# Layer 2's input projection taken of x times the scale, the norm's factor and the shift's product applied at its result

## The chip, the cores and the metric

The kernel runs on one core of a Trainium2 chip. The metric is device time in microseconds (us), of one launch. Engines are named as in the profile: PE (matrix multiply), PEld (PE's weight loads), DVE (vector), ACT (scalar with table functions), POOL (GpSimd), SP (the queue that issues most transfers).

## The reference

Two layers (`DEPTH` 2) over 1024 latent tokens and 256 context tokens, 1024 channels. What matters here is how a layer begins and what reads it:

```python
for l in range(DEPTH):
    sh1, sc1, g1, sh2, sc2, g2 = jnp.split(mod_l, 6, axis=-1)       # csh1, csc1, ... for the context
    hl = modulate(rms_norm(x, norm1[l]), sh1, sc1)
    hc = modulate(rms_norm(h_ctx, norm1[l]), csh1, csc1)
    y_l, y_c = token_mixers(hl, hc, ...)      # starts with hl @ w_in[l], hc @ w_in[l]
    x = x + g1 * y_l
    x = x + g2 * swiglu(modulate(rms_norm(x, norm2[l]), sh2, sc2), w_ffn_in[l], w_ffn_out[l])
    # the same for h_ctx, unless this is the last layer

qa, kva, kr, xr, gr, su, sv = split(h @ w_in)  # in token_mixers
```

`modulate(n, sh, sc)` is n (1 + sc) + sh, and `rms_norm` divides a token by the root of its mean square and multiplies by a gain. So the projection's operand is x · am · r + sh: `am`, the gain times (1 + sc), is one number per channel, `r` one per token, `sh` one per channel. From `qa` and `kva` (each normed again) come queries, keys and values of 10 heads; `xr` goes through a convolution, gates and a two-way recurrence; `gr` multiplies its result after a gelu; `su` and `sv` make a gated unit along the tokens.

## The kernel before

All arrays are fp32, and each is split into a high and a low part, so that a product is three matmuls: weights' high part (`wh`) with the operand's high and low part, and weights' low part (`wl`) with the high part. Channels lie on the 128 partitions, so x is 8 tiles (k or m) of tokens. A projection `prj` of 384 tokens is 24 matmuls of 384 columns (8 k by 3), one of 256 tokens 24 of 256.

The 1280 tokens are two chunks: chunk c=0 has tokens 0 to 640, c=1 the latent tokens 640 to 1024 (384 of them) and the 256 of the context; `SUBS` names the pieces, 384 and 256.

One program is written out by hand for all engines, with one queue per engine, in order. `pace(main)` runs a main generator, and each of its steps lets *lanes* (side generators, `Lane(gen, priority)`) go on; a model of engine clocks (`_Line`) decides how far. The order is fixed when the program is made. `ensure(condition)` runs lanes until a condition holds.

The end of layer 1 and the beginning of layer 2 (in the trace at 1646 to 1748 us):

- `ffn_rest(1, ...)`, the first pass: for each m, PE makes the last part of the feed-forward's result (`fr`, 512 latent columns and 256 of the context), DVE adds it to x (`x<-fr,g2h,x`), and `Running.add` has ACT square x (`sq`) and POOL add the squares over m; the last adds are on DVE. `ffn_rest(0, ...)`, the second pass, does the same for latent tokens 0 to 512.
- `rms_rinv`: three matmuls with ones (`ms`), then ACT (logarithm, exponential, square) and DVE (`v`, `v`, `r`) make `r`.
- `modulated`, in lanes: per k, DVE `ht` = x · am · r, ACT `h` high = `ht` + shift, DVE `h` low. There are 32 `ht` in this layer.
- `project`: PE's `prj` in the order `xr` (two output tiles of chunk 1, then two of chunk 0), `su`, `sv`, `kv`, `qa`, `gg` (the reference's gr). `sv` is made with h as the weights, so tokens lie on the partitions. ACT copies each result from PE's memory (`evac_copy`).

Behind `xr`, the recurrence (ACT gates, DVE scans) runs beside `su` and `sv`. Its last step, a DVE split of the next weights (`wl`) behind it and the first `kv` projection behind that, are at 1818.4. The low-rank norms of `kv` and `qa` (`acc`, `ms`, `v`, `r`, `kvf`, `qaf`, `qal`) lie among the `qa` and `gg` projections; then come k, v and q of the first pair of heads, and the first head's score maxima (`mx`) at 1902.5.

## Time and profile before

| | us |
|---|---|
| median of three runs | 3025.57 (3017.51 to 3028.01) |
| the profiled execution | 3020.45 |
| its span in the trace | 3018.7 |
| busy in it: PE, DVE, ACT, POOL | 2831.0, 2188.0, 1537.5, 927.5 |

The span is cut into stages by what PE does. A stage's own busy times, and what PE waits for in it, tell more than the shares of the whole span, since PE is busy almost all the time outside of a few stages.

### The profile page before, as it was taken

The numbers are of one execution on the slowest core, as the hardware profiler recorded it, in microseconds if no ns is written. First come the engines' busy times: TensorE is split into PE (matmuls) and PEld (weight loads), VectorE is DVE, ScalarE is ACT, GpSimd is POOL, SyncE is SP. The second block draws the span as 40 slices with busy tenths as digits, with TensorE's granted clock in tenths as the row PEclk, the third lists the DMA queues.
The fourth block names the chain that finished last, engine by engine and source line by source line (L and its number), as shares of the span: only waits on it lengthen the run. The fifth ranks groups of instructions, "written<-read, shape, count | busy, mean of one in ns | idle before, by whom it ended". The sixth has DMA issues, their size and how long they took to land.

```text
span 3018.7 us, 38935 instructions
## 1 busy us (share of the span) xinstructions
PE 2831.0 (94%) x13824; PEld 2316.2 (77%) x13824; DVE 2188.0 (72%) x3350; ACT 1537.5 (51%) x2846; POOL 927.5 (31%) x784
## 2 busy tenths in 40 slices
PE   6999999998899999999999799899999899999997
PEld 4788677777678788888888588577767688887886
DVE  5685777656688987776666767666756887777887
ACT  5665787874443333342112486578765544443223
POOL 0001366721223333332222200267712122222332
PEclk9999999999999999999999899999999899999999
DMA  7312000024144555558644211000024254446861
GB/s 279 127 32 78 25 18 1 1 98 156 41 149 160 187 178 199 178 186 305 258 155 152 87 47 50 25 8 8 1 96 156 67 174 150 150 150 246 326 248 66
DMA packets 150483, 378.65 MB, mean 125 GB/s; under 512 B 16016, under 2 KB 30352, under 8 KB 150288
## 3 DMA queue, kind: packets, MB, share of 16 engines
q1 hardware_dynamic: 147664, 367.24, 34.6%
q0 software_dynamic: 2624, 8.91, 0.8%
q8 instruction: 109, 1.79, 0.2%
q14 instruction: 86, 0.70, 0.1%
HBM read 270.19 MB, written 105.91 MB: 125 GB/s over the span
## 4 chain that ended last, share of the span: by engine, by line
PE 62%; DVE 14%; ACT 5%; DMA 3%; issue 2%; POOL 1%; DVEq 0%; POOLq 0%; ACTq 0%; SPq 0%
PE ffA L117 14%; PE foA L117 7%; PE ffC L117 6%; PE pv L117 5%; PE s L117 5%; PE ffB L117 3%; PE op L117 3%; PE foC L117 3%; PE prj L117 3%; DVE wl L117 2%; PE ffCU L117 2%; DVE x L117 2%; PE foX L117 2%; PE foB L117 2%; PE ffCG L117 2%
## 5 line engine op out<-in xcount | busy, mean ns | idle before, releaser
L117 DVE TENSOR_TENSOR wl<-wr,wh 128x512 fp32r<-128x512 f32 (+2 forms) x433 | 360.8, 835 | 152.6 <-ACT wh L117 150.1
L117 ACT CAST wh<-wr 128x512 fp32r<-128x512 f32 (+2 forms) x433 | 274.7, 651 | 381.4 <-PE foX L117 199.8
L117 PE MATMUL ffA<-T,wh 128*128 128x512 f32 x1056 | 334.7, 397 | 17.4 <-DVE e L117 9.1
L117 POOL TENSOR_TENSOR pl<-pf,ph 128x512 fp32r<-128x512 f32 (+1 forms) x231 | 308.7, 1346 | 137.7 <-ACT ph L117 110.5
L117 PE MATMUL prj<-h,wh 128*128 128x384 f32 (+1 forms) x1056 | 260.0, 334 | 18.5 <-ACT h L117 8.3
L117 ACT ACTIVATE pf<-s 128x512 f32<-128x512 f32 (+1 forms) x336 | 195.6, 588 | 114.6 <-PE s L117 109.8
L117 PEld LDWEIGHTS ffA<-T,wh 128*128 128x128 f32 x1056 | 199.3, 191 | 64.0 <-DVE T L117 12.3
L117 POOL TENSOR_TENSOR s<-wr 128x512 f32<-128x512 f32 (+1 forms) x84 | 93.7, 1116 | 415.2 <-DMA wr<-in_wfu_dram 191.2
L117 PEld LDWEIGHTS prj<-h,wh 128*128 128x128 f32 x1056 | 189.6, 199 | 40.6 <-DVE h L117 14.3
L117 DVE TENSOR_REDUCE mx<-mx 128x1 f32<-128x512 f32 (+1 forms) x328 | 202.9, 680 | 19.7 <-PE mx L117 19.1
L117 PE MATMUL ffA<-T,wl 128*128 128x512 f32 x528 | 208.1, 394 | 0.0
L117 ACT ACTIVATE th<-e 128x512 f32<-128x512 f32 x88 | 55.6, 632 | 272.6 <-DVE e L117 241.1
L117 PE MATMUL op<-y,wh 128*128 128x512 f32 (+1 forms) x576 | 182.6, 389 | 4.3 <-ACT y L117 2.0
L117 PE MATMUL prj<-h,wl 128*128 128x384 f32 (+1 forms) x528 | 170.9, 324 | 8.9 <-DVE wl L117 8.9
L117 DVE TENSOR_TENSOR wl<-s,wh 128x512 fp32r<-128x512 f32 (+1 forms) x168 | 158.4, 946 | 15.6 <-ACT wh L117 15.4
L117 POOL TENSOR_TENSOR sq<-sq,sq 128x512 f32<-128x512 f32 (+1 forms) x66 | 73.6, 1119 | 309.3 <-ACT sq L117 307.8
L117 POOL DMA_DIRECT2D ys<-y x20 | 11.1, 554 | 499.4 <-DVE y L117 498.6
L117 DVE SCALAR_TENSOR_TENSOR x<-foA,g2h,x 128x512 f32<-128x512 f32 x160 | 120.0, 750 | 60.4 <-PE foA L117 58.7
L117 PE MATMUL s<-qh,kh 97*128 97x512 f32 (+3 forms) x336 | 153.1, 456 | 4.0 <-ACT qh L117 1.8
L117 PE MATMUL foA<-T,wh 128*128 128x512 f32 x480 | 149.0, 392 | 6.4 <-DVE x L117 5.6
L117 ACT ACTIVATE ph<-s 128x512 fp32r<-128x512 f32 x242 | 141.6, 585 | 1.2 <-POOL qf L117 1.0
L117 PEld LDWEIGHTS op<-y,wh 128*128 128x128 f32 x576 | 109.3, 191 | 30.0 <-ACT wh L117 3.0
(348 smaller groups left out, 7889.3 us busy)
## 6 DMA issues: line engine op xcount, KB each, us to landing
wr<-in_wada_dram SPq DMA_DIRECT2D x80, 512.0 KB, 4.3
pair<-oh SPq DMA_DIRECT2D x140, 256.0 KB, 2.6
pair<-ol SPq DMA_DIRECT2D x140, 256.0 KB, 2.1
T<-pair SPq DMA_DIRECT2D x60, 512.0 KB, 9.3
wr<-in_wfg_dram SPq DMA_DIRECT2D x44, 512.0 KB, 4.1
wr<-in_wfu_dram SPq DMA_DIRECT2D x44, 512.0 KB, 5.2
wr<-in_wfo_dram SPq DMA_DIRECT2D x80, 256.0 KB, 5.0
B<-pair SPq DMA_DIRECT2D x40, 512.0 KB, 8.0
```

The lines of the kernel that those rows point to most:

```text
L117: return f(*args, **kw)
```

## The change

The high and low parts `h` of layer 2 are now made of x · am alone, by `Scaled`, inside the two passes of `ffn_rest`: one ACT operation (from x) and one DVE operation (x · am − high, with x and the high part as tensors), a step behind x. `ht` is gone. The token's factor `r` is kept in one tile `rn`. It is applied where a projection is read: DVE multiplies the result by `rn` (`pt`), and ACT adds the shift's product as a bias instead of copying. That product comes from two more columns of `h` (the shift of latent and context tokens) in the first piece of chunk 1, which is 386 columns wide; ACT copies it to `shifts`. For `sv` the factor has to lie on the partitions: ten small matmuls (`rt`) and two more `sv` tiles (`rows`, the shift's product spread over the partitions) are made, and DVE reads each tile with `stt` in place of ACT's copy. In the second pass the squares are added by DVE (`tt`), in the first still by POOL. `maxima` gives `mx` and `mr` three buffers of their own, and `next_pairs` waits for the values of the pair before.

```diff
     class Running:
         def add(self, k):
             sq = temp(name="sq")[:, : self.n]
             act(sq, x_at(k, self.g, self.n), AF.Square)
             self.flush()
...
-        def flush(self, add=gp.tensor_tensor):
+        def flush(self, add=None):
             if self.late is not None:
-                add(self.acc, self.acc, self.late, op=OP.add)
+                (add or self.how)(self.acc, self.acc, self.late, op=OP.add)
...
+    class Scaled:
+        def put(self, hs, k, pieces):
+            if len(hs) <= k:
+                hs.append(full((P, 2, CH + 2), R32, "h"))
+                if hs.second:
+                    h, b = hs[k][:, :, SHIFTS : SHIFTS + 2], self.mod[:, self.sh + k, 0:2]
+                    sc.copy(h[:, 0, :], b)
+                    self.late.append((tt, (h[:, 1, :], b, h[:, 0, :]), dict(op=OP.subtract)))
+            for at, n, g, w in pieces:
+                u = at_column(hs, at)
+                h, x, a = hs[k][:, :, u : u + n], x_at(k, g, n), self.am[:, k, w : w + 1]
+                act(h[:, 0, :], x, AF.Identity, scale=a)
+                self.late.append((stt, (h[:, 1, :], x, a, h[:, 0, :]), dict(op0=OP.mult, op1=OP.subtract)))
...
+            def late(ps, g, n):
+                if g == CH:
+                    sc.copy(shifts[:, of : of + 2], ps[:, n : n + 2])
+                t, v = temp(name="pt"), 0
+                while v < n:
+                    r, m = factor(g + v, n - v)
+                    tt(t[:, v : v + m], ps[:, v : v + m], r, op=OP.mult)
+                    v += m
+                k = of + int(g >= SEQ)
+                act(dst[:, g : g + n], t[:, :n], AF.Identity, bias=shifts[:, k : k + 1])
...
+                tiles[0:0] = [(2, 0), (2, 1)]
+                pt = psum("rt")
+                for i in range(10):
+                    r = factor(i * P, P)[0]
+                    mm(pt[:, 2 * i : 2 * i + 2], r, ones[:, 0:2], start=True, stop=True)
...
+                    if j < ntok[c]:
+                        stt(svs[c][:, j, :], ps[:, :256], q, rows[k][:, :256], op0=OP.mult, op1=OP.add)
+                    stt(krs[c][:, j, :], ps[:, -32:], q, rows[k][:, -32:], op0=OP.mult, op1=OP.add)
...
-        else:
-            Lane(modulated(h1[0], next_pieces, am1, mod, 0), 4)
...
-        norms, last_boxes = running(RESTP[1], not last)
-        pace(ffn_rest(1, norms))
...
+            norms0, boxes = running(RESTP[0], True, rn, tt)
...
+            def first_pass(i):
+                if i % 2 == 1:
+                    ys_of.flush()
+                    ys_of.put(h1[1], i // 2, [(0, SEQ - CH, CH, 0), (SEQ - CH, CTX, SEQ, 1)])
+            def second_pass(i):
+                ys_of.flush()
+                ys_of.put(h1[0], i, [(0, HT, 0, 0), (HT, CH - HT, HT, 0)])
+                if i in (1, 4):
+                    for r in norms.values():
+                        next(r.gen)
+            pace(ffn_rest(1, norms, first_pass))
+            pace(ffn_rest(0, norms0, second_pass))
```

What stands on the queues now, in three places (a name's number only tells one buffer from another).

DVE, the first pass. Before, two of its m:

```order
L117 SCALAR_TENSOR_TENSOR x_12877<-fr_15191,g2h_2958,x_12877 128x512
L117 SCALAR_TENSOR_TENSOR x_12880<-fr_15202,g2h_2958,x_12880 128x256
L117 SCALAR_TENSOR_TENSOR x_12877<-fr_15213,g2h_2958,x_12877 128x512
L117 SCALAR_TENSOR_TENSOR x_12877<-fr_15224,g2h_2958,x_12877 128x256
L117 SCALAR_TENSOR_TENSOR x_12900<-fr_15235,g2h_2958,x_12900 128x512
```

After, the same stretch:

```order
L117 SCALAR_TENSOR_TENSOR x_12887<-fr_15229,g2h_2962,x_12887 128x512
L117 SCALAR_TENSOR_TENSOR x_12890<-fr_15240,g2h_2962,x_12890 128x256
L117 TENSOR_TENSOR h_15225<-mod_109,h_15225 128x2
L117 SCALAR_TENSOR_TENSOR h_15225<-x_12881,am_15105,h_15225 128x384
L117 SCALAR_TENSOR_TENSOR h_15225<-x_12881,am_15105,h_15225 128x256
L117 SCALAR_TENSOR_TENSOR x_12887<-fr_15258,g2h_2962,x_12887 128x512
```

Three operations of `h`'s low part stand behind each pair of x; POOL's adds of the squares are as before.

DVE, from the end of the second pass to the first reading of a projection, after (`wl_15517` is the low part of the second weights of `xr`, `pt` the reading):

```order
L117 TENSOR_TENSOR sq_15355<-sq_15355,sq_15490 128x512
L117 SCALAR_TENSOR_TENSOR h_15479<-x_12913,am_15105,h_15479 128x512
L117 SCALAR_TENSOR_TENSOR h_15479<-x_12910,am_15105,h_15479 128x128
L117 SCALAR_TENSOR_TENSOR h_15496<-x_12913,am_15105,h_15496 128x512
L117 SCALAR_TENSOR_TENSOR h_15496<-x_12910,am_15105,h_15496 128x128
L117 TENSOR_TENSOR wl_15517<-wr_15038,wh_15516 128x1024
L117 TENSOR_TENSOR pt_15548<-prj_15522,rn_15104 128x384
```

The second weights' split stands behind everything that the second pass gives DVE. (The first weights' split, `wl_15423`, stands between the fourth and the fifth x of this pass.)

PE, from the last projection to the first head's keys. Before:

```order
L117 MATMUL ms_17174<-acc_17088,ones 128x384
L117 MATMUL ms_17181<-acc_17124,ones 128x256
L117 MATMUL prj_17188<-h_15524,wh_16925 128x256 x2
...
L117 MATMUL prj_17263<-h_15585,wh_17049 128x256 x2
L117 MATMUL prj_17263<-h_15585,wl_17050 128x256
L117 MATMUL k_17293<-kvh_15822,wqk_17138 128x512
```

After:

```order
L117 MATMUL prj_17281<-h_15496,wh_17073 128x256 x2
L117 MATMUL prj_17281<-h_15496,wl_17074 128x256
L117 MATMUL ms_17312<-acc_17240,ones 128x384
L117 MATMUL ms_17335<-acc_17328,ones 128x256
L117 MATMUL k_17350<-kvh_15798,wqk_17162 128x512
```

The last two norms of `qa` now stand between the last projection and the keys; before they stood ahead of three more projections.

## Rows read from the trace of the kernel before

**Rows 1.** Page, parts 1 and 4: PE's busy time; the chain by engine.

```profile
PE 2831.0 (94%) x13824; PEld 2316.2 (77%) x13824; DVE 2188.0 (72%) x3350; ACT 1537.5 (51%) x2846; POOL 927.5 (31%) x784
...
PE 62%; DVE 14%; ACT 5%; DMA 3%; issue 2%; POOL 1%; DVEq 0%; POOLq 0%; ACTq 0%; SPq 0%
```

**Rows 2.** Windows: us, busy PE, PEld, DVE, ACT, POOL, then PEclk, DMA.

```profile
1646.20:1676.10 29.90, 28.26 (x147) 23.61 (x145) 19.53 (x29) 12.15 (x22) 15.81 (x15) 1.00 0.10 36
...
1676.10:1692.50 16.40, 4.66 (x7) 1.85 (x6) 8.58 (x17) 8.15 (x15) 9.45 (x11) 0.71 0.82 292
...
1692.50:1739.70 47.20, 41.62 (x194) 34.10 (x195) 43.55 (x83) 23.35 (x43) 0.00 (x0) 0.81 0.15 46
...
1732.40:1739.50 7.10, 7.10 (x51) 7.10 (x50) 6.96 (x11) 1.80 (x3) 0.00 (x0) 1.00 0.24 65
...
1747.90:1818.40 70.50, 64.53 (x388) 55.52 (x386) 50.17 (x81) 63.77 (x106) 0.00 (x0) 0.96 0.11 36
...
1818.40:1889.70 71.30, 71.30 (x475) 68.28 (x476) 48.82 (x102) 45.04 (x92) 5.71 (x7) 0.97 0.17 56
...
1889.70:1902.50 12.80, 6.75 (x47) 5.89 (x45) 7.84 (x11) 8.56 (x19) 2.49 (x3) 0.96 0.00 0
```

**Rows 3.** Waits, 1640 to 1910: who, for whom, total us, times, longest.

```profile
DVE s L117 <- ACT q L117: 8.9, 1, 8.9
...
DVE w L117 <- ACT w L117: 7.3, 1, 7.3
...
PE prj L117 <- ACT h L117: 6.4, 2, 6.1
...
PE mx L117 <- ACT qh L117: 6.1, 1, 6.1
...
PE ms L117 <- DVE sq L117: 5.7, 1, 5.7
...
PE prj L117 <- DVE h L117: 4.0, 7, 2.1
```

**Rows 4.** Timeline of DVE and POOL: start, us, what ran, idle before.

```profile
939.98 1.61 POOL L117 TENSOR_TENSOR s<-s,wr 128x512 f32<-128x512 f32 x1
...
940.37 1.77 DVE L117 TENSOR_TENSOR wl<-wr,wh 128x512 fp32r<-128x512 f32 x1
...
1655.60 10.39 POOL L117 TENSOR_TENSOR sq<-sq,sq 128x512 f32<-128x512 f32 x10 [0.17 <-ACT sq L117]
...
1656.14 1.20 DVE L117 SCALAR_TENSOR_TENSOR x<-fr,g2h,x 128x512 f32<-128x512 f32 x2 [0.90 <-PE fr L117]
...
1658.24 1.20 DVE L117 SCALAR_TENSOR_TENSOR x<-fr,g2h,x 128x512 f32<-128x512 f32 x2 [0.90 <-PE fr L117]
...
1670.40 4.04 POOL L117 TENSOR_TENSOR sq<-sq,sq 128x512 f32<-128x512 f32 x3 [4.41 <-ACT sq L117]
...
1673.18 2.34 DVE L117 TENSOR_TENSOR wl<-wr,wh 128x1024 fp32r<-128x1024 f32 x1 [1.70 <-ACT wh L117]
...
1707.56 1.23 DVE L117 TENSOR_TENSOR wl<-wr,wh 128x1024 fp32r<-128x1024 f32 x1 [0.45 <-ACT wh L117]
```

**Rows 5.** Timeline of DVE, 1681 to 1719: one piece of each kind.

```profile
1681.04 0.69 DVE L117 TENSOR_TENSOR sq<-sq,sq 128x512 f32<-128x512 f32 x1 [2.88 <-POOL sq L117]
...
1693.56 0.61 DVE L117 SCALAR_TENSOR_TENSOR h<-ht,mod,h 128x384 fp32r<-128x384 f32 x1
...
1717.99 0.74 DVE L117 SCALAR_TENSOR_TENSOR h<-ht,mod,h 128x512 fp32r<-128x512 f32 x1
```

**Rows 6.** Groups by shape, 1740 to 1818: busy us, mean ns of one.

```profile
L117 ACT COPY sv<-sv 128x256 f32<-128x256 f32 x8 | 2.9, 364 | 1.6 <-PE sv L117 1.6
...
L117 PE MATMUL sv<-wl,h 128*128 128x288 f32 x48 | 14.9, 310 | 0.0
```

**Rows 7.** Timeline of ACT and DVE around the low-rank norms.

```profile
1879.42 0.58 ACT L117 ACTIVATE r<-ms,eps 128x384 f32<-128x384 f32 x1 [0.17 <-PE ms L117]
...
1881.14 0.56 DVE L117 SCALAR_TENSOR_TENSOR v<-ms,v 128x384 f32<-128x384 f32 x1
```

More of the change, by code (lines that the diff above doesn't have):

```diff
@@ L519, in rms_rinv @@
         yield [acc]
-        r, v = (temp(name=x)[:, :n] for x in "rv") if work is None else work[1:]
+        r, v = (temp(name=x)[:, :n] for x in "rv") if work is None and to is None else work[1:] if to is None else (to, temp(name="v")[:, :n])
         ps = psum("ms")[:, :n]
@@ L693, in add, with running @@
                     self.gen = gen
-        def flush(self, add=gp.tensor_tensor):
+        def flush(self, add=None):
             if self.late is not None:
-                add(self.acc, self.acc, self.late, op=OP.add)
+                (add or self.how)(self.acc, self.acc, self.late, op=OP.add)
                 self.late = None
-    def running(pieces, lane=True):
-        norms = {g: Running(g, n, lane) for g, n in pieces}
+    def running(pieces, lane=True, to=None, add=gp.tensor_tensor):
+        norms = {g: Running(g, n, lane, to, add) for g, n in pieces}
         return norms, {g: r.box for g, r in norms.items()}
@@ L719, in modulated @@
                 if len(hs) <= k:
-                    hs.append(full((P, 2, CH), R32, "h"))
+                    hs.append(full((P, 2, CH + 2), R32, "h"))
                 h = hs[k]
@@ L735, in hybrid_block_kernel, with __init__ @@
     class Normed(list):
-        def __init__(self):
+        def __init__(self, second):
             super().__init__()
-            self.done = set()
+            self.done, self.second = set(), second
     lconst = {}
@@ L2353, in ffn_rest @@
             order = [(m, *at) for m in range(KT) for at in RESTP[c]]
-            if beside is not None:
+            if last:
                 order.sort(key=lambda piece: piece[1])
@@ L2378, in ffn_rest @@
                         beside(done)
-                    elif c == 0 and m == KT - 1:
-                        early[0] = 2.0
                     yield
-                if c == 0 and beside is None and m % 4 == 3:
+                if c == 0 and not last and m % 4 == 3:
                     wrest[m // 4] = None
```

129 lines of the change are left out of this document (85 added, 44 removed).

## The prediction

> **What bounds the kernel now.** I read the page first: PE is busy 94% of the span and makes 62% of the chain that ended last [rows 1]. So work taken off another engine is worth something only where PE waits, and I went on to windows, cut where PE's work changes, and to the waits there. The change touches the stretch from 1646 to 1902 us. In it PE has three gaps [rows 2, 3]:
>
> - Between the end of the feed-forward passes (1676.1) and the first projection (1692.5) PE does 4.66 us in 16.4 at a granted clock of 0.71. It waits 5.7 for DVE's last sum of squares and then 6.1 (of 6.4) for ACT's `h`.
> - In the `xr` projections (1692.5 to 1739.7) it is busy 41.6 of 47.2 at 0.81. It waits 4.0 for DVE's `h`, and runs slowly behind each gap. DVE is busy 43.6 of the 47.2: it sets the pace.
> - From 1747.9 to 1818.4 PE is busy 64.5 of 70.5, while ACT is busy 63.8: this is the recurrence. It ends on DVE, in whose queue the next weights' split stands. DVE has idle time only early there, 8.9 and 7.3 waiting for ACT [rows 3].
>
> From 1818.4 to 1889.7 PE is busy throughout, and what follows to 1902.5 is a fixed chain (keys, values, queries, ACT's `qh`) with a wait of 6.1. The change aims at the first two gaps: about 12 + 5.6 = 17 us is all that they hold.
>
> **First pass.** PE gives a pair of x every 2.10 us (DVE's pairs start at 1656.14 and 1658.24 [rows 4]). DVE now needs per m: the pair 1.20, the two columns about 0.12 (my estimate, for the shortest kind of operation), the low parts 0.53 and 0.42 (a 384 piece starts 0.53 before the next, though its row says 0.61 [rows 5]; the 256 one by its length). Together 2.27: alone that is level with PE. But POOL adds squares beside it, ten in 10.39 us, nearly without a pause. The x pair is not touched by that: 1.20 while POOL runs. An operation with two tensors from the SBUF is: `wl` of 512 took 1.77 beside POOL's add at 939.98 and ended when that did, and `wl` of 1024 took 2.34 at 1673.18 beside three adds, against 1.23 at 1707.56, when POOL was idle [rows 4]. The low part of `h` is such an operation (x and the high part). POOL's adds are 2.0 per m. If the x pair lies beside one add and the low parts wait for the rest, DVE takes 3.1 to 3.5 per m; I take 3.3, which is 1.04 more than 2.27 in seven m, 7.3 us. DVE starts the pass at about 1650, so it ends it at 1650 + 8 × 2.27 + 1.5 (the first weights) + 7.3 = 1677.
>
> The Trainium skill, "SBUF — State Buffer", section "Who interferes with whom", says that a DVE instruction with two SBUF inputs contends with a POOL instruction that reads the SBUF, and that the second one blocks fully for the length of the first. The rows above agree in kind. Read strictly, nothing of the two would overlap; the sum is then that of the second rival.
>
> **Second pass.** Here DVE does all, per m: x 0.70, square's add 0.69 [rows 5] less an overlap of 0.07, low part 0.66 + 0.27. That is 2.28, while PE needs at most (29.9 − 8 × 2.1) / 8 = 1.6 per m [rows 2]. So DVE sets it: 18.2, with the first pass's norm (two pieces, 2.9), two weight splits (1.15 each) and about 3.3 in which ACT makes that norm instead of squares. DVE ends at 1677 + 18.2 + 2.9 + 2.3 + 3.3 = 1704. PE finds the first weights after four of the eight m, at 1677 + 9.1 + 1.2 + 2.2 = 1689.5 instead of 1692.5; the second weights only at 1704, since their split is last in DVE's queue. A pair of pieces, 384 and 256, takes 7.1 at full clock [rows 2]; the first pair lies in between, slowly. From 1704 the other three pairs are 21.3, and 3 for a slow clock after the gap: `xr` is done at 1728.3, 11.4 earlier than 1739.7. So of the 17 us the change gets two thirds; the rest turns into a wait for `wl`. Bounds: 7.3 us earlier if nothing is lost beside POOL, 7 later if all is.
>
> **To the recurrence's end.** Before, two pieces of `su` (8.2 us) stood ahead of the first gates. Now there are three and a small `ms`, 12.0. The gates start at 1740.3, 7.6 earlier. What is new in the phase: on PE two `sv` tiles, 48 matmuls of 288 columns at some 0.134 us from start to start, 6.4 (the rows' mean of 310 ns [rows 6] contains the overlap), and ten `rt` at most 2.5; on DVE the readings of `sv` and `kr`, 8 × 0.42 + 10 × 0.17 = 5.1, and some `pt` pieces at 0.42 to 0.56 (by `v<-ms,v`, which reads PE's memory [rows 7]), of which I count 2.6 in the solid part. ACT loses 8 × 0.36 = 2.9 of `sv` copies [rows 6]. The 16 us of DVE waits early in the phase take up what stands early; in the rest DVE was solid. Of 7.7 on DVE about 5.8 falls into its idle time, so I charge 1.9; the ends are 0 and 8.9 (all of PE's work bare). The first `kv` projection is then at 1740.3 + 70.5 + 1.9 = 1812.7, 5.7 earlier.
>
> **To the first scores.** PE's 71.3 stay. Then the change takes something back: two `qa` norms stand between the last projection and the keys. From that end: `pt` 0.6, ACT's reading 0.35, three ACT steps at 0.56 (1.7), DVE's three (1.5) and the scaling of two `qaf` (1.1), ACT's `qah` and squares (1.8), DVE's sum 0.5, `ms` 0.9: 8.5 (steps of the kind of [rows 7]). Keys, values and queries used to start at once; the chain of 12.8 behind stays. First scores: 1812.7 + 71.3 + 8.5 + 12.8 = 1905.3 against 1902.5, a loss of 2.8.
>
> **The rest.** The merging of `su` (six DVE adds of at most 0.69 [rows 5] and what follows them) falls from the projections into the first head. PE is the bound there; I charge 1, between 0 and the adds' 4. The order in layer 1's first heads changes slightly, at nothing: PE's cover is whole, and ±1.5 if it is not. The own buffers of `mx` and `mr` and the removal of 32 `ht` cost nothing.
>
> **Sum.** −11.4 (xr) + 3.8 (one more `su` piece ahead) + 1.9 + 8.5 + 1 = +3.8. The profiled execution took 3020.45 (1.75 around its span); so it would be 3024. That execution lies 5.1 below the median of the runs, and against the median the forecast is 3029. About 0.3%, 9 us, is what a measurement here can tell from no change: this is no change.
>
> **Rivals.**
> 1. *The boundary closes.* Operations with x and the high part run beside POOL undisturbed, and the squares and norms hide behind PE. For it: most of this work is short, and PE has less to do. Against it: the `wl` rows, and the 2.28 to 1.6 of the second pass. The price: the whole 17 instead of 11.4, a further 6, and with 1.9 for the recurrence, half of the 8.5 and the 1 of the heads saved as well, 3.8 − 6 − 1.9 − 4.3 − 1 = −9.4: 3016. Chance 0.23. It decides if `xr` is done by 1722.
> 2. *DVE and POOL in strict turn* in the first pass: the low parts wait for both adds, 2.27 + 2.0 = 4.3 per m instead of 3.3. For it: POOL is never idle there, so every low part finds an add running. Against it: `wl` at 1673.18 lost 1.1 to three adds, not 4. The price is 7 × 1.0, a total of +11: 3036. It is slower once the pass costs over 4.1 per m. Chance 0.13.
> 3. *The readings decide.* PE's results wait in its memory for a DVE that is in the scans. For it: DVE was solid from 1780 to 1817. Against: 16 us of idle before. The price: 8.9 instead of 1.9, and 2 in the heads: 3038. It is slower once the phase from the gates to `kv` is over 76. Chance 0.17.
> 4. *The change doesn't do what it says*: the projections still wait for something, now `wl`, and nothing is gained at the boundary: that is partly in the sum; whole, it is +11, 3040. Chance 0.04.
>
> **Numbers.** The forecast has 0.43, and its bounds are those of the terms: 3020 to 3034. Faster has rival 1 and a little of the forecast's low end: 0.24; slower rivals 2 to 4: 0.33; the same 0.43. For 8 in 10 the range goes to 3012 and 3041.
>
> **What would show it.** In the trace after: low parts of `h` in the first pass longer than 0.8 us; the second pass's x about 2.3 apart; PE waiting for a `wl` between the second and third `xr` piece; the first gates 6 to 9 us earlier against the start of the passes; a PE gap of about 8 ahead of the keys. The forecast is wrong if the low parts are 0.6, or if the gates-to-`kv` phase grows by more than 5.

## The result: 41 us slower, and where they are

The changed kernel takes 3067.23 us (median of four runs, 3062.5 to 3068.64) against 3026.36 for the kernel before beside it (3017.51 to 3028.01): ratio 1.0137, interval 1.0123 to 1.0150. The forecast was 3029, with a range to 3041: no change. The time lies above the range.

The page of the kernel after, parts 1 and 4, answers to [rows 1]:

```profile
PE 2872.4 (94%) x13894; PEld 2327.4 (76%) x13894; DVE 2202.2 (72%) x3391; ACT 1539.2 (50%) x2850; POOL 921.7 (30%) x778
...
PE 71%; DVE 17%; ACT 7%; issue 3%; DMA 3%; SPq 0%; POOL 0%; DVEq 0%; POOLq 0%; ACTq 0%
```

PE is busy 41 us longer, for 70 more matmuls of 13,824. A busy PE that has grown by as much as the span says: look for matmuls that became slower, not only for waits. So I divided both traces at the first matmul of each kind and compared the lengths of the stages. The table is worked out from the timelines of PE; `op` is the output projection behind the heads, `fr` the first matmul of the feed-forward passes at the boundary of the layers, and "`kv` resumed" the `kv` projection behind PE's wait for its weights' split.

| stage, from .. to | before | after | difference | forecast |
|---|---|---|---|---|
| start .. first maxima (`mx`), layer 1 | 292.5 | 294.5 | +2.0 | 0 |
| heads, layer 1: `mx` .. `op` | 357.8 | 363.3 | +5.5 | 0 |
| `op` .. `fr` | 996.0 | 1002.0 | +6.0 | 0 |
| boundary and `xr`: `fr` .. first gates (`zr`) | 101.5 | 91.8 | −9.7 | −7.6 |
| recurrence: `zr` .. `kv` resumed | 70.6 | 77.9 | +7.3 | +1.9 |
| `kv` .. first maxima, layer 2 | 84.1 | 93.6 | +9.5 | +8.5 |
| heads, layer 2: `mx` .. `op` | 330.2 | 342.2 | +12.0 | +1 |
| `op` .. end of PE's last matmul | 776.1 | 789.2 | +13.1 | 0 |
| sum | | | +45.7 | +3.8 |

The stages come from one execution each; those at the front move by 2 to 4 us between executions of one kernel, and the recurrence by up to 3 with the granted clock (below). The two that the forecast worked out most closely, the boundary and the stretch ahead of the keys, are right to 2 us. The 41.9 between forecast and measurement lie in the recurrence (5.4), in the heads of both layers (16.5) and in stretches that the change does not touch (21.1); the boundary and the keys together give 1.1 back.

The windows of the kernel after: first pass, second pass, `xr`, recurrence, `kv` to the last projection, keys, heads, and a stretch of layer 2's feed-forward. Columns as in [rows 2], which the first six answer to.

```profile
1659.80:1684.00 24.20, 20.00 (x110) 16.66 (x108) 22.95 (x37) 14.63 (x36) 12.68 (x12) 1.00 0.14 44
1684.00:1699.70 15.70, 11.57 (x40) 8.16 (x40) 10.98 (x23) 11.95 (x24) 4.84 (x7) 0.89 0.54 201
1699.70:1751.60 51.90, 46.83 (x267) 45.11 (x267) 39.66 (x69) 18.69 (x33) 1.37 (x2) 0.87 0.26 84
1751.60:1829.50 77.90, 68.89 (x431) 59.96 (x431) 56.77 (x105) 63.47 (x92) 0.00 (x0) 0.96 0.09 28
1829.50:1899.00 69.50, 68.88 (x467) 66.82 (x468) 39.67 (x89) 33.76 (x70) 1.69 (x2) 0.97 0.15 48
1908.10:1923.10 15.00, 8.77 (x47) 7.49 (x46) 9.74 (x15) 11.76 (x26) 2.27 (x3) 0.84 0.00 0
1923.10:2265.30 342.20, 325.79 (x1328) 244.24 (x1329) 226.00 (x324) 250.37 (x450) 184.00 (x147) 0.96 0.05 16
...
2449.80:2810.70 360.90, 360.90 (x1557) 292.23 (x1556) 281.16 (x364) 159.87 (x290) 105.67 (x76) 1.00 0.45 157
```

The same heads and the same feed-forward stretch in the kernel before:

```profile
1902.50:2232.70 330.20, 317.58 (x1325) 240.62 (x1325) 213.04 (x308) 245.39 (x439) 184.51 (x144) 0.98 0.04 13
...
2418.00:2771.00 353.00, 353.00 (x1559) 292.31 (x1558) 281.50 (x364) 159.08 (x290) 105.72 (x76) 1.00 0.47 160
```

The last row of each is the surprise. Nothing in that stretch was edited, PE waits for nothing, and the granted clock is 1.00 in both, yet the same matmuls take 360.9 us instead of 353.0.

The waits of the kernel after, 1640 to 1930, answer to [rows 3]:

```profile
PE prj L117 <- DVE wl L117: 10.3, 3, 8.6
...
DVE w L117 <- ACT w L117: 8.3, 1, 8.3
...
PE ms L117 <- DVE acc L117: 7.8, 1, 7.8
...
PE mx L117 <- ACT qh L117: 6.2, 1, 6.2
...
PE ms L117 <- DVE sq L117: 4.8, 1, 4.8
...
PE prj L117 <- ACT shifts L117: 2.9, 1, 2.9
...
PE prj L117 <- ACT wh L117: 1.9, 1, 1.9
```

One of the kernel before, 1640 to 1910, stands beside the first of them:

```profile
PE prj L117 <- DVE wl L117: 4.5, 2, 3.9
```

Of PE's waits at the boundary in [rows 3], the one for `sq` is 4.8 instead of 5.7, and 1.9 for `wh` has taken the place of 6.1 for `h`. The 2.9 for `shifts` (PE waits until a result has been read) is new; the wait for the second `wl`, which was forecast there, is 1.1 behind it. The wait for a weight split behind the recurrence is 8.6 (3.9 before), and 7.8 for the `qa` norm ahead of the keys is new.

### The profile page after: what moved, and what is told of

It reads as the page before. It is cut to its first block, busy times and chain, and to the rows that moved or that the text cites. A ratio compares the mean times of both kernels' runs of the same rounds, so it can differ in the third digit from the quotient of the medians.

```text
span 3064.4 us, 39134 instructions
## 1 busy us (share of the span) xinstructions
PE 2872.4 (94%) x13894; PEld 2327.4 (76%) x13894; DVE 2202.2 (72%) x3391; ACT 1539.2 (50%) x2850; POOL 921.7 (30%) x778
## 4 chain that ended last, share of the span: by engine, by line
PE 71%; DVE 17%; ACT 7%; issue 3%; DMA 3%; SPq 0%; POOL 0%; DVEq 0%; POOLq 0%; ACTq 0%
PE ffA L117 15%; PE prj L117 7%; PE foA L117 7%; PE ffC L117 7%; PE pv L117 6%; PE s L117 5%; PE op L117 4%; PE ffB L117 3%; PE foC L117 3%; DVE mx L117 3%; DVE x L117 2%; PE ffCU L117 2%; DVE wl L117 2%; PE foB L117 2%; PE foX L117 2%
## 5 line engine op out<-in xcount | busy, mean ns | idle before, releaser
L117 PE MATMUL prj<-h,wh 128*128 128x256 f32 (+2 forms) x1056 | 253.0, 330 | 11.6 <-ACT wh L117 3.5
L117 PE MATMUL prj<-h,wl 128*128 128x256 f32 (+2 forms) x528 | 171.2, 324 | 14.6 <-DVE wl L117 14.6
L117 DVE TENSOR_TENSOR wl<-s,wh 128x512 fp32r<-128x512 f32 (+1 forms) x168 | 155.1, 927 | 14.5 <-ACT wh L117 14.2
L117 POOL TENSOR_TENSOR sq<-sq,sq 128x512 f32<-128x512 f32 (+1 forms) x60 | 67.1, 1123 | 308.5 <-ACT sq L117 307.8
L117 ACT ACTIVATE ph<-s 128x512 fp32r<-128x512 f32 (+1 forms) x244 | 142.5, 584 | 1.2 <-POOL qf L117 1.0
L117 PE MATMUL mx<-kh,qh 128*128 128x512 f32 (+3 forms) x400 | 114.2, 401 | 20.1 <-ACT qh L117 12.1
```

The source lines that it names most:

```text
L117: return f(*args, **kw)
```

## Experiments: matmuls that became slower

First I looked at where tiles lie. Two columns more per operand tile make all 28 large tiles 5152 bytes long instead of 5120 (rows of 5136, rounded to 32), and smaller tiles of the change shift what follows them. **b_shift** is the kernel before with everything moved by 32 bytes; **a_shift** is the changed kernel with small tiles packed so that the weights start on multiples of 64 again:

```diff
+    pad = cp.tile([P, 8], F32, name="pad")
```

> The kernel before with one unused constant of 32 bytes ahead of the others, so that every weights, temps and full tile starts 32 bytes past a multiple of 64 instead of on one; the order on every engine is the same. In the trace of after, the feed-forward stretches that the change does not touch have no wait on PE in either trace, yet 353.0 us before are 360.9 after (2.2%), and the last one 195 us grows by 5.2. Theory address: PE pays for the start of its operands, so this kernel is slower by 12 to 30 us, and the 353.0 stretch becomes about 361. Rival (the drift comes with the order or with the run): within 0.3% of before, and the stretch stays at 353.

```diff
-    eps = cp.tile([P, 1], F32, name="eps")
...
+    eps = czs[:, 47:48]
```

> The kernel after with 32 bytes less of constants (the small constant eps moved into the unused end of another constant), so that weights and temps start on multiples of 64 bytes again; of the full tiles every second one still starts 32 past one. The order on every engine is that of after. Theory address, by the weights: the 360.9 stretch returns to 353 and the whole to about 3067 - 16 = 3051. If the full tiles (the moving operands) are what counts, only half of it returns, about 3059. Rival: 3067, as after.

b_shift: 3023.87 against 3023.91, ratio 1.0000 (0.9990 to 1.0009); its feed-forward stretch takes 353.4. a_shift: 3065.92, ratio 1.0142 (1.0125 to 1.0159), as the changed kernel. A common shift neither costs nor mends anything. a_shift is the base of most later runs. Runs that leave something out (a_640 aside) and a_tail were executed once each.

**b_stride** is the kernel before with its large tiles 5152 bytes apart (small tiles are packed to make room; a few rows in the heads change places), **a_640** is a_shift without the two columns and so with tiles 5120 apart:

```diff
-                    hs.append(full((P, 2, CH), R32, "h"))
+                    hs.append(full((P, 2 * CH + 4), R32, "h")[:, 0 : 2 * CH].rearrange("p (a b) -> p a b", a=2))
```

> The kernel before, whose h tiles have four columns more at their end that nothing uses, so that the large tiles stand 5152 bytes apart, as in after, instead of 5120; two small constants are packed tighter to make room. The order on every engine is that of before. Theory stride: what slows PE's matmuls in after (353.0 us becoming 360.9 without a wait) is how the large tiles lie to each other, since a shift of all by 32 bytes did nothing. Then this kernel is 12 to 20 us slower than before. Rival (something else of after's program): within 0.3% of before.

```diff
-                hs.append(full((P, 2, CH + 2), R32, "h"))
...
+                hs.append(full((P, 2, CH), R32, "h"))
```

> The kernel a_shift without the two columns for the shift: h has 640 columns as before, the large tiles stand 5120 bytes apart, and the 386-column projections have 384; the shift's product is then read from a wrong column (of the result itself) and the eight small copies are left out. Theory stride: the untouched feed-forward of layer 2 takes 353 instead of 361 and the whole gains 12 to 20 us, to about 3050. Rival: 3065 as a_shift, less about 1 for the columns.

b_stride: 3051.99 against 3020.70, ratio 1.0100 (1.0085 to 1.0115). a_640: 3051.42, ratio 1.0102 (1.0086 to 1.0119), 14.5 below a_shift, or 12 by the two ratios, since each run has its own runs of the kernel before beside it. (The trace of a_640 is of an execution of 3043.71.) In a_640 the feed-forward stretch is back at the kernel before's 353:

```profile
2440.00:2793.00 353.00, 353.00 (x1559) 292.31 (x1558) 280.55 (x364) 159.08 (x290) 105.89 (x77) 1.00 0.46 160
```

So 12 to 15 us of the loss go with the longer tiles, that is with addresses; a_wide below keeps the two columns and bears this out. What about the addresses? **b_alt** moves every second large tile by 32 bytes (5120 apart otherwise), **b_phase** moves all large tiles (and what lies behind them) by 32 bytes against the weights and the raw buffers, and **a_wide** is the complete changed kernel with 20 large tiles 5120 and 8 tiles 5184 apart, all on multiples of 64:

```diff
-    fp = ctx.enter_context(tc.tile_pool(name="full", bufs=28))
+    fps = [ctx.enter_context(tc.tile_pool(name="full", bufs=14))]
+    gap = ctx.enter_context(tc.tile_pool(name="gap", bufs=1)).tile([P, 8], F32, name="gap")
+    fps.append(ctx.enter_context(tc.tile_pool(name="full2", bufs=14)))
```

> The kernel before, with its 28 large tiles in two groups of 14 with 32 free bytes between them, and the tiles dealt to the groups so that every second one of the old places is in the second group: within a group the starts stay 5120 bytes apart, and half of the large tiles start 32 bytes past a multiple of 64, as they do with starts 5152 bytes apart. The order of the instructions is the same. The run with starts 5152 bytes apart took 3051.99 us against 3020.70 (ratio 1.0100). Theory A, that it is the half of the tiles off the multiples of 64, alone or beside the others, that slows TensorE's matmuls: about 3050 us, ratio 1.009 to 1.011, and the stretch of the last feed-forward products 8 us longer than before's 353.0. Theory B, that it is the distance from tile to tile (each a further 32 bytes on), not which half of a 64-byte block a tile starts in: ratio 0.999 to 1.002, the stretch at 353.

```diff
-    fp = ctx.enter_context(tc.tile_pool(name="full", bufs=28))
+    fps = [ctx.enter_context(tc.tile_pool(name=x, bufs=n)) for x, n in (("full", 20), ("wide", 8))]
...
+        t = fps[pool].tile([P, 1296] if pool else list(shape), dt, tag="f", name=nm(name))
```

> The changed kernel, complete, with 20 large tiles 5120 bytes apart and 8 tiles 5184 bytes apart, so that every large tile starts on a multiple of 64 bytes and the 8 operand tiles with the shift columns lie in the wider ones; the order of the instructions is the same. Theory A, that starts off the multiples of 64 slow TensorE's matmuls: 3050 to 3054 us, ratio 1.009 to 1.0105, and the stretch of the last feed-forward products back at 353 us. Theory B, that any mixture of distances does it, or the shift columns themselves (386 columns instead of 384): 3063 to 3068 us, ratio 1.013 to 1.015, and the stretch at 361.

```diff
+    gap = ctx.enter_context(tc.tile_pool(name="gap", bufs=1)).tile([P, 8], F32, name="gap")
...
     fp = ctx.enter_context(tc.tile_pool(name="full", bufs=28))
```

> The kernel before with 32 free bytes between the weights and the large tiles: all large tiles stay 5120 bytes (five times 1024) apart, so they start alike modulo 1024, but 32 bytes further than the weights do. Order the same. Theory W, that a moving operand that starts elsewhere modulo 1024 than the weights is slow: the stretch of the last feed-forward products about 361 us instead of 353, ratio 1.005 to 1.010. Theory T, that it is a change of the place from one operand tile to the next: the stretch at 353, ratio 0.999 to 1.002.

b_alt: 3038.55, ratio 1.0052 (1.0035 to 1.0069). a_wide: 3053.47, ratio 1.0096 (1.0081 to 1.0111), 12.5 below a_shift (14 by the ratios). b_phase: 3045.68, ratio 1.0064 (1.0039 to 1.0089). (Its four executions took 3038.29 to 3054.89; the trace is of the last named.) The order of instructions is the same in each pair, so a matmul of the feed-forward stretch can be set beside its operand's address in the compiled program. Each of 28 operand tiles is read there by three matmuls in a row (two with `wh`, one with `wl`), 18 or 19 times; the table gives the least and the largest of the 28 means, from the first start to the start of the next three:

| kernel | where the operand tiles start, against the weights, modulo 1024 bytes | three matmuls, ns |
|---|---|---|
| before | all 28 at the same place | 680 |
| b_phase | all 28 by 32 bytes further | 699 to 702 |
| b_alt | 14 at the same place; 14 by 32 further | 680 to 696; 689 to 703 |
| a_wide | 21 at the same place; 7 by 64 to 448 further | 680 to 698; 691 to 703 |
| b_stride | 1 at the same place, 27 at as many distances | 696; 687 to 705 |

The groups by shape over that stretch show it too, as lengths of single matmuls (neighbours overlap, so a length is more than a step). Kernel before, then b_phase:

```profile
L117 PE MATMUL ffA<-T,wh 128*128 128x512 f32 x448 | 138.0, 389 | 0.0
```

```profile
L117 PE MATMUL ffA<-T,wh 128*128 128x512 f32 x448 | 140.8, 395 | 0.0
```

b_phase decides it: its large tiles stand to one another as before, and their place against the weights has changed. With all operands at the weights' place a matmul of 512 columns takes 226.7 ns, with all 32 bytes beside it 233, and the stretch takes 364.3 at a granted clock of 1.00. b_shift fits: there weights and operands moved together. The raw buffers lie at the same place modulo 1024 as the weights, so the place against them is not separated from the place against the weights.

Where the places are mixed, a tile's own distance does not fix its time. In b_alt the tiles at the weights' place take up to 696 behind one that lies 32 further, and are back at 680 only as the third or fourth of an unbroken row (695, 690, 680, 680 and 696, 696, 684, 680). In the kernel after, the one tile at the weights' place takes 698, and one that lies 512 bytes off takes 680. Multiples of 64 are not enough: in a_wide the stretch takes 357.5, and the whole stage to the output products (from the first `ffA` to the first `foA`) is still 4.4 us longer than before, against 8.2 in a_shift. Theory A of b_alt and a_wide, that starts off the multiples of 64 are slow, therefore names the wrong boundary, though some of its figures came out (a_wide's time, b_alt's stretch with 362.3); others did not (b_alt's ratio, and 353 for a_wide's stretch). Why the place matters is not shown.

## Experiments: the boundary

**a_noadd** is a_shift without POOL's adds of squares in the first pass (these sums are left out):

```diff
-                (add or self.how)(self.acc, self.acc, self.late, op=OP.add)
+                if add or self.how is not none:
+                    (add or self.how)(self.acc, self.acc, self.late, op=OP.add)
```

> The kernel a_shift with POOL's adds of the squares in the first pass left out (the norm of the latent tokens from 512 on and of the context is then of the wrong sum); nothing else moves. Theory lock: an h low part of DVE (x and the high part as tensors) waits for POOL's add; without the adds the pairs of x stand 2.3 us apart instead of 3.08, the pass ends about 7 x 0.8 = 5.6 us earlier, and the low parts take 0.6 instead of 0.7 to 1.3. Rival: DVE's own work sets 3.08, nothing moves.

It took 3057.74 in one run; the first projection comes 6.2 us earlier. DVE's timeline of the kernel after (start, length), then POOL's, then DVE's of a_noadd:

```profile
1668.61 1.13 DVE L117 SCALAR_TENSOR_TENSOR x<-fr,g2h,x 128x512 f32<-128x512 f32 x2
...
1671.70 1.13 DVE L117 SCALAR_TENSOR_TENSOR x<-fr,g2h,x 128x512 f32<-128x512 f32 x2
...
1682.61 1.48 DVE L117 SCALAR_TENSOR_TENSOR h<-x,am,h 128x256 fp32r<-128x256 f32 x1
```

```profile
1670.16 2.21 POOL L117 TENSOR_TENSOR sq<-sq,sq 128x512 f32<-128x512 f32 x2 [0.87 <-ACT sq L117]
```

```profile
1668.43 1.19 DVE L117 SCALAR_TENSOR_TENSOR x<-fr,g2h,x 128x512 f32<-128x512 f32 x2
1669.61 1.01 DVE L117 SCALAR_TENSOR_TENSOR h<-x,am,h 128x384 fp32r<-128x384 f32 x2
1670.53 1.19 DVE L117 SCALAR_TENSOR_TENSOR x<-fr,g2h,x 128x512 f32<-128x512 f32 x2
```

Beside POOL the pairs of x are 3.09 apart, without it 2.10, which is PE's own step. The low part of 256 takes 1.48: one of POOL's adds (half of 2.21) and its own 0.4. It waits for one add, not for both.

## Experiments: the recurrence

From the first gates to `kv` the kernel after is 7.3 us longer, a_shift and a_640 8.2. The difference between these two goes with the granted clock. In traces with the order of after the stage takes 77.8 to 77.9 us where the clock is 1.00 up to PE's wait at the end (after, a_wide), 78.6 to 78.8 where 3.4 us ahead of that wait lie at its lower level of 1.2 GHz (a_shift, a_640, a_tail, a_nomerge) and 79.4 to 79.5 with 6.8 us (a_noadd, a_nosu). With the order of before it takes 70.6 in four traces, with 3.4 to 6.8 us at the lower level, and 73.8 in two, b_gatemp and b_phase, with 13.7. This is the stretch of b_phase; PE was busy 41.5 of the 42.1 us ahead of it, at 1.00:

```profile
1798.90:1812.60 13.70, 13.70 (x52) 11.63 (x52) 13.32 (x20) 10.88 (x18) 0.00 (x0) 0.50 0.00 1
```

So with at most 6.8 us at the lower level the loss is 7.3 to 8.9 us, and the clock is not what makes it. Three suspects were taken away, each in its place in the order. **a_svact** lets ACT read the spatial part's tiles, scaled, without adding the shift rows:

```diff
-                    stt(krs[c][:, j, :], ps[:, -32:], q, rows[k][:, -32:], op0=OP.mult, op1=OP.add)
...
+                            nc.scalar.activation(out, ps[:, u], AF.Identity, scale=q)
```

> The kernel a_shift in which ACT reads the sv tiles of layer 2, scaled by the token's factor, at the place where DVE did; the shift's product is not added to them. The rest of the order is the same. Theory readings (rival 3 of the prediction): DVE waits in the recurrence for sv tiles that PE has not finished (1.2, 2.5 and 0.8 us in one trace) and the reads cost it 5 more, so the first kv projection comes 7 to 10 us earlier. Rival (PE's two more tiles set the phase): under 2 us earlier.

**a_notile** issues only the first and the last matmul of the two shift tiles:

```diff
-                part(pss[c, j], terms, blocks[0] == 0, blocks[-1] == 2)
...
+                        if (blocks[0] == 0 and i == 0) or (blocks[-1] == 2 and i == len(all3) - 1):
+                            mm(ps, w, h, start=i == 0 and blocks[0] == 0, stop=i > 0)
```

> The changed kernel with large tiles 5120 bytes apart (as in the run without the shift columns), and of the two shift tiles' matmuls in the second layer's spatial part only the first and the last of each are issued, 46 left out; the order of all else is kept. What is left out: most of the products of the two shift rows, so their values are wrong. The time from the recurrence's first product to the next projection was 8.2 us longer than before in both the changed kernel and the one without shift columns. Theory P, that TensorE's two more tiles are what is late there: that stage falls to +1 to +3 us, the sum by 5 to 7 us. Theory V, that it is the later and longer readings on VectorE and ScalarE: it stays at +6 to +9 us, and TensorE waits for them instead.

**a_noread** cuts DVE's product with the norm's factor to 8 columns, and ACT reads PE's result itself:

```diff
-                    tt(t[:, v : v + m], ps[:, v : v + m], r, op=OP.mult)
...
+                    nc.vector.tensor_tensor(t[:, v : v + 8], ps[:, v : v + 8], r[:, :8], op=OP.mult)
```

> The changed kernel with large tiles 5120 bytes apart, and in the second layer's readings VectorE's product with the norm's factor is cut to 8 columns and ScalarE reads TensorE's result itself and adds the bias, so that a reading costs VectorE next to nothing and no longer goes through two engines. What is left out: the product with the norm's factor, except for the spatial part's tiles. Order kept. Without the two shift tiles' matmuls the recurrence's stage had still been 7.3 us longer than before. Theory V, that the readings through VectorE are late there: the stage falls from 8.2 to +1 to +4 us, and the keys' stage (11.3 us longer) by 1 to 3. Theory W, that the order of the gates' products, the scans and the spatial tiles is the loss, whoever reads: the stage stays at +6 to +8 us.

The stage stays 7.0, 7.3 and 8.8 us longer (whole runs: 3065.73, 3047.58, 3048.28). None of the three alone is it, also with the clock allowed for: 3.4 us at the lower level in a_svact, 6.8 in a_notile and a_noread, so by the lengths above I estimate that the three give back 1.1, 1.6 and nothing. PE's timeline of a_notile shows where some time of the missing matmuls goes:

```profile
1773.95 1.12 PE L117 MATMUL zi<-xc,gates 128*128 128x512 f32 x2 [2.96 <-ACT s L117]
```

PE reaches the gates' products earlier and waits there for ACT's `s`. What it could do meanwhile, the token tiles of `sv`, stands behind the gates in its queue. That led to another theory. The order has three `sv` tiles begun ahead of the gates. Before, these were tiles of tokens; now two of the three are shift tiles, and two token tiles stand behind. **a_ends4** begins four early (two of tokens); **a_onerow** has one shift tile and begins four (three of tokens, as before):

```diff
-            ends = tiles[:3], tiles[-3:]
+            ends = tiles[: 4 if l > 0 else 3], tiles[-3:]
```

> The changed kernel with large tiles 5120 bytes apart, and in the second layer four spatial tiles instead of three begun early (two thirds of their products, ahead of the recurrence's gate products). In the kernel before the three early ones are tiles of tokens; in the changed one two of the three are the shift tiles, so that only one tile of tokens is early and two more stand behind the gates' products. Theory E, that this place is the recurrence's loss: with two tiles of tokens early the stage falls from 8.2 to +4 to +6.5 us, the sum by 2 to 4 us. Theory W, that it is not the place of the tiles: the stage stays at +7 to +9.

```diff
-                tiles[0:0] = [(2, 0), (2, 1)]
+                tiles[0:0] = [(2, 0)]
...
-            ends = tiles[:3], tiles[-3:]
+            ends = tiles[: 4 if l > 0 else 3], tiles[-3:]
```

> As the run before, and one shift tile instead of two (what is left out: the context's shift row, for which the latents' is used), so that three tiles of tokens are begun early, as in the kernel before. Theory E: the recurrence's stage falls from 8.2 to +1 to +4 us, 2 to 4 below the run with two early. Theory W: it falls by what the one tile's matmuls cost at most, to +5 to +8.

a_ends4 stays at +7.7 (3045.86); a_onerow falls to +2.7, and the whole to 3030.00. Two early token tiles do next to nothing; three, with one shift tile less, do most. And a_onerow gains more than that stage: the keys, queries and heads behind it are 9.9 us longer than before in sum instead of a_640's 21.0. Its order of rows also differs in these stages, so this run alone does not show which part of it is the tile's place and which the new order. The clock is not it: up to the wait that ends the recurrence it is 1.00, as in the kernel after, with its 77.9 against 73.3. Its window up to that wait, and PE's waits from 1720 to 1920:

```profile
1743.30:1814.10 70.80, 65.83 (x406) 56.76 (x406) 49.30 (x91) 61.13 (x89) 0.00 (x0) 1.00 0.07 23
```

```profile
PE mx L117 <- ACT qh L117: 6.9, 1, 6.9
PE prj L117 <- DVE wl L117: 6.8, 1, 6.8
...
PE ms L117 <- DVE acc L117: 3.1, 1, 3.1
```

## Experiments: the norm ahead of the keys, and the heads

**a_tail** puts the second `qa` norm ahead of the last projection:

```diff
+                        if l > 0 and c == 0 and i == 1 and s0 > 0:
+                            ensure(lambda: ranked[C_QAN] >= 2)
```

> The kernel a_shift in which the second of the three qa norms is made ahead of the last projection instead of behind it; the third stays. Theory tail: PE waits 7.8 us ahead of the keys since each norm's chain begins where the one before it ended; with one of them hidden the keys come 3 to 5 us earlier. Rival: the chain begins with the last projection's reading anyway, and nothing is gained.

3065.31; PE's wait ahead of the keys is still there, 8.0 us. The last piece's norm, not the second, is what the keys wait for.

**b_gatemp** is the kernel before with two small edits of the change: the next pair's keys wait for the values of the pair ahead, and the maxima have their own buffers.

```diff
-                yield lambda: current[0] >= 2 * p - 2 and l in conditioned
+                yield lambda: current[0] >= 2 * p - 2 and l in conditioned and (p % 2 or len(valued) >= 2 * p)
```

> The kernel before with two small parts of the change alone, both in the heads and in both layers: the next pair's keys and values wait until the values of the pair ahead are split (the added condition with the list of split values), and the maxima have their own buffers. In the changed kernel and in the run with its large tiles 5120 bytes apart the heads took longer in both layers (from first maxima to output projection 5.4 and 12.1 us, 4.3 and 9.7 us), though layer 1 computes the same as before. Theory G, that the later keys and values of the next pairs are the loss there: heads +4 to +6 in layer 1 and +7 to +10 in layer 2, the whole 3033 to 3039, ratio 1.003 to 1.005. Theory L, that layer 2's heads are late because its projections end in another order, and layer 1's differ by chance: 3021 to 3027, ratio 0.999 to 1.002.

3028.00 against 3022.79, ratio 1.0019 (1.0009 to 1.0028). Layer 1's heads take 4.2 us longer, layer 2's 0.2 less. So the two edits are most of layer 1's loss of 5.5, and none of layer 2's. It is the condition: a_best below keeps the buffers and drops the condition in layer 1, and its heads there are +0.7. Both theories were half right.

**a_nosu** and **a_nomerge**, on a_640, cut the norm of the spatial part's output, and then of the recurrence's too, to 8 columns of 512 on each engine (the rest of these norms is left out).

```diff
+                left = l > 0 and k0 == 2
+                yield from (rms_narrow if left else rms_rinv)([s[:, e] for s in srcs], n, d, box)
```

> The changed kernel with large tiles 5120 bytes apart, and in the second layer the norm of the spatial part's output cut to 8 of its 512 columns per piece on ScalarE, VectorE and TensorE (the rest of the norm is left out); the outputs are still written, by one scalar factor. Order kept. In the changed kernel this norm runs among the heads (1935 to 1974 us), before it ran ahead of them. The heads' stage was 9.7 us longer than before there. Theory N, that the norm's work between the heads' maxima is the loss: the stage falls to +1 to +4 us. Theory O, that it is the heads' own order and their later queries, not this norm: it stays at +7 to +10 us.

```diff
-                left = l > 0 and k0 == 2
+                left = l > 0
```

> The changed kernel with large tiles 5120 bytes apart, and in the second layer the norms of both the spatial part's and the recurrence's output cut to 8 of 512 columns per piece on all engines (the rest of these norms is left out; the outputs are written, by one factor). Order kept. With the spatial part's alone cut the heads were 8.8 us longer than before. In the kernel before, the recurrence's norm is among the heads too, so this takes away a little more than the change added. Theory N, that the norms beside GpSimd's work are the heads' loss: +0 to +4. Theory O, that the loss is the order of the heads' own steps and the clock: +6 to +9.

The heads of layer 2 are 8.8 and 3.7 us longer than before, against 9.7 in a_640; the whole runs took 3043.38 and 3035.17. So up to 6 of the 9.7 go with these two norms (at most, since the kernel before too has the recurrence's norm among its heads, and the stage takes 339.8 to 341.7 in the traces with a_640's layout and order behind the recurrence). Most of it is waiting: PE is idle 12.6 us in these heads before, 18.4 in a_640 and 14.0 in a_nomerge. DVE's groups by shape among the heads, of a_640 (busy, mean ns, idle), then of the kernel before:

```profile
L117 DVE TENSOR_TENSOR acc<-acc,sq 128x512 f32<-128x512 f32 x4 | 4.8, 1194 | 1.3 <-ACT sq L117 1.3
...
L117 DVE SCALAR_TENSOR_TENSOR y<-rec,cols,r 128x512 f32<-128x512 f32 x4 | 3.9, 1006 | 0.1
```

```profile
L117 DVE SCALAR_TENSOR_TENSOR y<-rec,cols,r 128x512 f32<-128x512 f32 x4 | 2.8, 749 | 0.1
...
L117 DVE TENSOR_TENSOR acc<-acc,sq 128x512 f32<-128x512 f32 x2 | 1.4, 693 | 1.8 <-ACT sq L117 1.8
```

Before, the spatial part's norm was done among the projections and the recurrence's in the first heads. Now both come some 60 to 90 us later, beside POOL's work for the heads (low parts of the attention weights, `pl`, 1.3 us and more each, and `qf`), and the same operation takes 1.19 us instead of 0.69. Two groups of a_nomerge show that the length is waiting, not work: eight columns take twice what 512 do undisturbed. Of the four in the first row, the three that lie beside an operation of POOL take 0.95 to 1.21, and the one that does not takes 0.17.

```profile
L575 DVE TENSOR_SCALAR v<-v 128x8 f32<-128x8 f32 x4 | 3.5, 876 | 0.1
...
L117 DVE TENSOR_SCALAR v<-v 128x512 f32<-128x512 f32 x1 | 0.4, 427 | 0.0
```

But the place among the heads is not the whole cause. a_onerow has both norms there as well, with DVE as busy (224.5 us, as in a_640), and its heads are only 1.3 us longer than before; none of its adds is lengthened (0.68 to 0.69). In the kernel after only one of the four adds and one of the four `y` are long (1.76 and 1.78), and its heads are 12.0 longer. By its row above PE is busy 8.2 of these 12.0 longer, at a granted clock of 0.96 instead of 0.98, and idle 3.8 longer: part of the loss is again slower matmuls, by address or by clock. How the rest divides was not taken apart.

## Experiments: the findings together

**a_best** is the complete changed kernel with what the runs found: large tiles as in a_wide, one shift tile that holds both rows (the context's in 32 columns), three token tiles early, and the added condition in layer 2 alone.

```diff
-                tiles[0:0] = [(2, 0), (2, 1)]
+                tiles[0:0] = [(2, 0)]
+                rows = [rowt[:, :NSV], rowt[:, NSV : NSV + 32]]
-                yield lambda: current[0] >= 2 * p - 2 and l in conditioned and (p % 2 or len(valued) >= 2 * p)
+                yield lambda: current[0] >= 2 * p - 2 and l in conditioned and (l == 0 or p % 2 or len(valued) >= 2 * p)
```

> The changed kernel, complete, with large tiles on multiples of 64 bytes as in the run before, one shift tile in the second layer that holds both rows (the latents' in 288 columns, the context's in the 32 that are read of it), three tiles of tokens begun early as in the kernel before, and the added condition on the next pairs' keys in the second layer alone. Theory E, that the early tiles' place decides the recurrence, the keys and the heads behind it: 3022 to 3032 us, ratio 0.999 to 1.0025. Theory F, that the run with one shift tile was fast because its keys, by chance of the order, came earlier, and another order loses it again: 3036 to 3050 us.

3035.83 against 3024.05, ratio 1.0040 (1.0026 to 1.0054): 31 us faster than the change (29 by the ratios), and still slower than before. By its trace layer 1's heads are +0.7 and the keys start without the wait; but the recurrence is +6.3 and layer 2's heads +9.3. So three early token tiles are not the whole of a_onerow's gain: with the context row's 24 matmuls in the tile the planner laid out another order. A part is the clock: a_best has 6.8 us at the lower level in the recurrence, with PE busy throughout, and a_onerow none ahead of its last wait. By the traces above (77.9 to 79.5) I estimate 1.6 of the 3.5 us between the two runs for it.

```profile
1790.60:1797.40 6.80, 6.80 (x31) 6.80 (x31) 6.46 (x10) 6.71 (x10) 0.00 (x0) 0.50 0.01 2
```

The theory of the place (E) fits a_onerow and fell here; which order of gates, token tiles and norms would keep a_onerow's gain stays open.

## Why the prediction was wrong, step by step

**First pass: right.** 3.3 us per m was forecast, 3.09 measured, and 2.10 without POOL (2.27 forecast). The Trainium skill, "SBUF — State Buffer", section "Who interferes with whom", says that a DVE instruction with two SBUF inputs contends with a POOL instruction that reads the SBUF; the low part's 1.48 next to 1.1 for one add agrees. The second rival (two adds per m) fell. The `wl` row of [rows 4] had shown as much: it ended at 942.14, 0.55 after POOL's add, and not with it, as I read it. No row gave the 0.12 for the two columns; the trace after has 0.14.

**Second pass and `xr`: right.** The gates start 9.7 us earlier than before, counted from the start of the passes; 7.6 was forecast. In the second pass x stands 2.2 apart (2.3 forecast; my 2.28 is 2.25 by its own terms). The wait inside `xr` is in a new place, 2.9 for `shifts` and then 1.1 for `wl`.

**The recurrence: the term of 1.9 was mis-sized; it is 7.3.** (The forecast had named a growth by more than 5 as a sign of being wrong.) The third rival named its threshold (over 76; it is 77.9) and its price (8.9), but a wrong mechanism: without DVE's readings the stage stays 8.8 longer. My sum counted PE's and DVE's added work and looked for idle time to hide it. It did not ask what the added tiles push back in PE's queue. That this is the cause is the reading that a_onerow suggests; a_best does not bear it out, and the cause stays open.

**Ahead of the keys: right.** 8.5 forecast, 7.8 waited, 9.5 for the whole stage.

**The heads: mis-sized, 1 against 12.0, and 0 against 5.5.** "PE is the bound there" was my cover for the norms. PE's idle time there grew from 12.6 to 16.4 us and its busy time from 317.6 to 325.8, so the cover was not whole, and PE's own work did not keep its length. Up to 6 of a_640's 9.7 go with the two norms, whose operations last up to 2.5 times as long beside POOL (1.76 instead of 0.69). For layer 1 I had set ±1.5 for a changed order, without working out the added condition: it delays the next pair's keys, 4.2 us in b_gatemp.

**The step that is not in the sum: the addresses, 12 to 15 us.** I counted the two columns only as columns that are read. They lengthen 28 buffers, and matmuls become slower in stretches that the change does not touch (360.9 instead of 353.0 us). This alone moves the forecast out of "no change".

Together: 3029 + 5.4 + 11.0 + 5.5 for the three terms and 12 to 15 for the addresses is 3063 to 3066. Some of this is counted twice: a_640, whose tiles are as long as before, loses 9.7 and 4.3 in the heads and not 12.0 and 5.5. So the sum comes near the 3067 with some luck.

**Not settled:** how layer 2's heads lose what the norms leave, which order the recurrence needs, and why the addresses matter.

## What to carry to other kernels

Compare the granted clock and PE's time per matmul in a stretch that the change does not touch: if the clock is the same and the time differs, look at the addresses, and ask of every tile that grows how its pool's other tiles come to lie. When work is added to a full queue, look also at what it moves behind the next wait, not only at its own length: leaving out 46 of the added matmuls gave back some 1.6 of 8 us here. Price an operation that is moved into a stretch where POOL works by rows from there, not from its old place (0.69 and up to 1.76 us for the same add here).

## What the runs showed of the hardware

Three matmuls of 512 columns take 680 ns where all large tiles start at the same place modulo 1024 bytes as the weights (the columns that are read then start level with the weights' columns or 512 bytes off), and 699 to 702 where all start 32 bytes further, at the same granted clock of 1.00 and with no wait: 3%, and 0.6 to 1.0% of this kernel (b_phase 1.0064, b_stride 1.0100). The Trainium skill, "SBUF — State Buffer", section "Who interferes with whom", lists TensorE's two read ports, one for the moving operand and one for the weights, as independent. In b_phase the operands, and the small buffers behind them, lie 32 bytes further from the weights and the raw buffers, and the matmuls are slower; whether the two reads meet there is not shown by any run.
